# One of the four weight-block sums of each seven-product FFN pair: made by GpSimd instead of VectorE

## The chip, the core and the metric

The kernel runs on one core of one Trainium2 chip. The metric is the device time of one execution in microseconds (us). Engines go by their short names: PE is TensorE, which multiplies matrices (PEld is its weight load), DVE is VectorE, ACT is ScalarE, POOL is GpSimd, and SP is SyncE, which only issues transfers here.

## The reference, cut to what matters

The program is one layer of an encoder: 256 tokens, model width 2048, float32. After two kinds of attention comes a feed-forward network (FFN) with a gate, and it is the FFN that the change touches:

```
D_MODEL = 2048; SEQ = 256; D_FF = 5632
h = layer_norm(DEEPNORM_ALPHA * h + mixed, ln1_g[l], ln1_b[l])
ffn = jnp.einsum('bsf,fd->bsd', jax.nn.silu(jnp.einsum('bsd,df->bsf', h, w_gate[l]))
                 * jnp.einsum('bsd,df->bsf', h, w_up[l]), w_down[l])
h = layer_norm(DEEPNORM_ALPHA * h + ffn, ln2_g[l], ln2_b[l])
```

`w_gate` and `w_up` are 2048 x 5632, `w_down` is 5632 x 2048. All 5632 columns of gate and up, less one strip of 512 that is done ahead, belong to the part that the change touches.

## The kernel before, in words

**Products in two halves.** A float32 number is split into a rounded part (`hi`, type fp32r, made by ACT as a copy) and the rest (`lo`, made by DVE as the difference). A product of two float32 blocks is then three matmuls: hi by hi, hi by lo, lo by hi. So each weight block needs one ACT copy and one DVE subtraction before PE can use it.

**Units, groups and pairs.** The weights come in units of 128 rows x 1024 columns (`raw[u]`, half a MB, one SP transfer each). The FFN's gate and up matrices are walked in groups of 16 units: ("g", j) for gate and ("u", j) for up, j from 0 to 4, each 1024 columns wide. Within a group two neighbouring units make a pair, seen as 2 x 2 blocks of 128 x 512. Eight pairs make a group. A normal pair is eight products of three matmuls. In the four pairs of a group named by `SEVEN = (0, 2, 4, 6)` the 2 x 2 product is done in the manner of Strassen and Winograd with seven products instead of eight; these need sums of weight blocks first. There are 10 groups and so 40 seven-pairs in gate and up. The down projection (groups ("d", n)) comes behind them and has seven-pairs of its own.

**What a seven-pair asks of the engines** (`seven_parts(u)`; r1 and r2 are the two raw units):

- t1 (DVE): first half of the tile `s["t"]` = r1 left + r1 right, 128 x 512
- t3 (DVE): second half of `s["t"]` = r1 right + r2 right, 128 x 512
- lo11 (DVE, 512 columns), behind ACT's hi11
- t24 (DVE): two sums of 512 columns, the second on top of the first; the first reads t1's half alone
- lo2 (DVE, 1024 columns) behind ACT's split_hi of r2
- hi13 (ACT): one copy of both halves of `s["t"]`, 1024 columns; lo13 (DVE, 1024 columns) behind it
- hi24 (ACT) and lo24 (DVE), 1024 columns, for the t24 sums

A normal pair asks DVE for two `lo` of 1024 columns. At the end of a group DVE also joins the products out of PSUM (`ffn_ends`, `block_end`); for an "up" group it multiplies gate by up (tiles `s`), PE transposes the result, ACT copies it (`nb`) and POOL issues the transfer to `mid_d`.

**What sets the order.** Instructions are put out at build time by a planner: `Timed` keeps a modelled clock for each engine, and `next_part` gives the next ready part of a pair to the engine that its `op(...)` entry names. At run time each engine works through its list in order and waits for semaphores. What is ready early is kept in 46 slots of 4 KB per partition (tiles named `sl`). `Engine.__getattr__` issues every operation, so all of them carry line 53 in the profile.

Of the kernel before, what the change touches and what calls it, by code (L numbers as in the profile page):

```python
# [12 lines left out]
ALU = mybir.AluOpType  # L13
# [239 lines left out]
def layer_kernel(ctx: ExitStack, tc: tile.TileContext, A: dict, out: bass.AP):  # L253
    nc = Timed(tc.nc)
# [17 lines left out]
    def slot(shape, dt=F32):  # L272
        t = slab.tile(shape, dt, tag="slab", name=nm("sl"))
        if len(taken) + len(left_over) >= SLOTS and left_over:
            old = min(left_over, key=lambda x: nc.idle(x))
            left_over.remove(old)
            nc.follows(t, old)
        taken.append(t)
        return t
# [5 lines left out]
    def leave(*tiles):  # L285

        for t in tiles:
            taken.remove(t)
            left_over.append(t)
# [3 lines left out]
    def used(key, n, *tiles):  # L293

        uses[key] = uses.get(key, 0) + 1
        if uses[key] == n:
            leave(*tiles)
# [109 lines left out]
    def split_hi(u):  # L407
        wh[u] = slot([P, 1024], F32R)
        nc.scalar.activation(wh[u], raw[u], AF.Copy)

    def split_lo(u):
        wl[u] = slot([P, 1024], F32R)
        nc.vector.tensor_tensor(wl[u], raw[u], wh[u].bitcast(F32), op=ALU.subtract)
# [590 lines left out]
    def op(engine, fn, reads=(), after=(), early=False, takes=0):  # L1004


        return dict(engine=engine, fn=fn, reads=reads, after=after, early=early, takes=takes, done=False)
# [13 lines left out]
    def seven_parts(u):  # L1021

        r1, r2 = raw[u], raw[u + 1]
        s = sums[u] = {}

        def t1():
            s["t"] = slot([P, 2, 512])
            nc.vector.tensor_tensor(s["t"][:, 0], r1[:, :512], r1[:, 512:], op=ALU.add)

        def t3():  # L1030
            nc.vector.tensor_tensor(s["t"][:, 1], r1[:, 512:], r2[:, 512:], op=ALU.add)

        def hi11():
            s["b11"] = slot([P, 2, 512], F32R)
            nc.scalar.activation(s["b11"][:, 0], r1[:, :512], AF.Copy)

        def lo11():
            nc.vector.tensor_tensor(s["b11"][:, 1], r1[:, :512], s["b11"][:, 0].bitcast(F32), op=ALU.subtract)
            leave(r1)

        def hi13():
            s["hi"], s["lo"] = slot([P, 2, 512], F32R), slot([P, 2, 512], F32R)
            nc.scalar.activation(s["hi"], s["t"], AF.Copy)

        def lo13():
            nc.vector.tensor_tensor(s["lo"], s["t"], s["hi"].bitcast(F32), op=ALU.subtract)
            used(("t", u), 2, s["t"])

        def t24():
            s["u"] = slot([P, 2, 512])  # L1050
            nc.vector.tensor_tensor(s["u"][:, 0], s["t"][:, 0], r2[:, 512:], op=ALU.add)
            nc.vector.tensor_tensor(s["u"][:, 1], s["u"][:, 0], r2[:, :512], op=ALU.add)
            used(("t", u), 2, s["t"])
            used(("r2", u), 2, r2)

        def hi24():
            s[2], s[4] = slot([P, 2, 512], F32R), slot([P, 2, 512], F32R)
            nc.scalar.activation(s[2], s["u"], AF.Copy)

        def lo24():  # L1060
            nc.vector.tensor_tensor(s[4], s["u"], s[2].bitcast(F32), op=ALU.subtract)
            leave(s["u"])

        def lo2():
            split_lo(u + 1)
            used(("r2", u), 2, r2)

        return [
            op("act", hi11, lambda: [r1], takes=1),
            op("dve", t1, lambda: [r1], takes=1),  # L1070
            op("dve", t3, lambda: [r1, r2], (1,)),
            op("act", lambda: split_hi(u + 1), lambda: [r2], takes=1),
            op("dve", lo11, lambda: [s["b11"][:, 0]], (0, 1, 2)),
            op("act", hi13, lambda: [s["t"]], (1, 2), takes=2),
            op("dve", t24, lambda: [s["t"]], (1, 2), takes=1),
            op("dve", lo2, lambda: [wh[u + 1]], (3,), takes=1),
            op("act", hi24, lambda: [s["u"]], (6,), takes=2),
            op("dve", lo13, lambda: [s["hi"]], (5,)),
            op("dve", lo24, lambda: [s[2]], (8,)),
        ]  # L1080
# [54 lines left out]
    def is_down(u):  # L1135
        return units[u]["group"][0] == "d" and isinstance(units[u]["group"], tuple)
# [314 lines left out]
    def prepare(u, seven):  # L1451

        if u not in stages:
            stages[u] = seven_parts(u) if seven else one_parts(u)
            if splits_mid(u):
                add_mid_split(u, stages[u])
            if seven and is_down(u):
                add_mid_sums(u, stages[u])
        return stages[u]
# [165 lines left out]
```

## Time and profile before

| | us |
|---|---|
| time, median of 3 runs (1127.65 to 1128.34) | 1127.96 |
| profiled execution, its own time | 1127.88 |
| its span, first to last instruction | 1126.1 |
| PE busy | 1111.5 |
| DVE busy | 929.0 |
| ACT busy | 598.9 |
| POOL busy | 57.7 |

The span is the part of an execution that the trace covers; the profiled execution took 1.78 us more than its span. "Busy" adds up the time in which at least one instruction of the engine was running. The shares are means over stages that differ: the gate and up groups lie between about 452 and 856 us, the down projection behind them. The granted TensorE clock was 0.999 of full speed over the span, that is its upper level of 2.4 GHz.

### The profile page before, as it was taken

The page shows a single profiled execution, that of the slowest core. Times are in us where ns is not written, and L with a number is a line of the kernel's source. Part 1 is how long each engine was busy: PE and PEld are TensorE (multiplying, and loading weights), DVE is VectorE, ACT ScalarE, POOL GpSimd, SP SyncE. Part 2 cuts the span into 40 slices and gives each one's busy share as a digit, 9 for nine tenths or more (in the row PEclk, how much of TensorE's full clock was granted, in tenths as well). Part 3 has the DMA queues.
Part 4 walks back from the last instruction along what each step waited for, and adds up shares of the span by engine and source line. Part 5 has one row for each costly group of instructions (what it writes and reads, how often), then busy time and mean ns, then how long its engine had stood idle before and what let it go on. Part 6 is the DMA issues. An engine that isn't in the chain of part 4 may idle for free.

```text
span 1126.1 us, 14151 instructions
## 1 busy us (share of the span) xinstructions
PE 1111.5 (99%) x5032; PEld 904.7 (80%) x5032; DVE 929.0 (83%) x1263; ACT 598.9 (53%) x785; POOL 57.7 (5%) x110
## 2 busy tenths in 40 slices
PE   8999999999999999999999999999999999999998
PEld 4788888888788876888888888888888788878885
DVE  7863876547773669999999999999999999799865
ACT  5552656435563228656556556556567566446640
POOL 2000003110100020000000000000000000000000
PEclk9999999999999999999999999999999999999999
DMA  9664548795766754655754755755756877667741
GB/s 345 233 202 157 166 145 166 183 205 190 159 220 229 243 183 135 211 195 174 269 205 165 278 204 164 280 193 177 271 208 222 286 266 279 218 225 283 250 166 75
DMA packets 70407, 237.15 MB, mean 211 GB/s; under 512 B 8516, under 2 KB 9924, under 8 KB 70336
## 3 DMA queue, kind: packets, MB, share of 16 engines
q1 hardware_dynamic: 65008, 220.49, 57.2%
q0 software_dynamic: 5168, 15.68, 6.8%
q8 instruction: 39, 0.64, 0.2%
q14 instruction: 32, 0.26, 0.1%
q10 hardware_dynamic: 160, 0.08, 0.0%
HBM read 226.25 MB, written 9.97 MB: 210 GB/s over the span
## 4 chain that ended last, share of the span: by engine, by line
PE 49%; issue 41%; DVE 4%; ACT 2%; POOL 2%; DMA 1%; POOLq 0%; ACTq 0%; DVEq 0%
PE acc L53 49%; DVE sl L53 3%; POOL mid_d L53 1%; ACT sl L53 1%; DMA mid_d<-nb 1%; DVE stats L53 1%; ACT s L53 1%; DMA ident<-in_c_ident_dram 0%; DVE s L53 0%; POOL h_d L53 0%; POOL rs L53 0%; DMA sl<-in_w_out_dram 0%; POOL rstd L53 0%; ACT o L53 0%; DVE o L53 0%
## 5 line engine op out<-in xcount | busy, mean ns | idle before, releaser
L53 PE MATMUL acc<-sl,sl 128*128 128x512 f32 (+1 forms) x4676 | 1063.0, 388 | 2.3 <-DVE sl L53 1.4
L53 PEld LDWEIGHTS acc<-sl,sl 128*128 128x128 f32 x4676 | 860.5, 188 | 184.1 <-issue 6.2
L53 DVE TENSOR_TENSOR sl<-sl,sl 128x1024 fp32r<-128x1024 f32 (+3 forms) x710 | 683.1, 1017 | 44.9 <-ACT sl L53 36.6
L53 ACT ACTIVATE sl<-sl 128x1024 fp32r<-128x1024 f32 (+1 forms) x530 | 498.6, 994 | 272.8 <-DVE sl L53 140.8
L53 ACT ACTIVATE sl<-acc 128x256 fp32r<-128x256 f32 (+2 forms) x70 | 33.1, 497 | 91.0 <-PE acc L53 72.4
L53 DVE TENSOR_TENSOR sl<-acc,sl 128x256 fp32r<-128x256 f32 (+2 forms) x94 | 54.8, 596 | 28.2 <-ACT sl L53 21.5
L53 DVE TENSOR_TENSOR sl<-sl 128x512 f32<-128x512 f32 (+1 forms) x76 | 41.4, 558 | 0.3 <-PE acc L53 0.3
L53 DVE SCALAR_TENSOR_TENSOR sl<-sl,acc 128x512 f32<-128x512 f32 x10 | 6.8, 679 | 36.6 <-PE acc L53 36.6
L53 POOL DMA_DIRECT2D mid_d<-nb x22 | 11.9, 540 | 459.1 <-ACT nb L53 459.1
L53 ACT COPY sl<-acc 128x512 f32<-128x512 f32 x31 | 17.1, 588 | 34.3 <-PE acc L53 34.3
L53 ACT COPY nb<-acc 128x512 f32<-128x512 f32 x24 | 14.1, 588 | 35.1 <-PE acc L53 30.3
L53 DVE TENSOR_SCALAR sl<-acc 128x512 f32<-128x512 f32 x8 | 5.5, 688 | 32.7 <-PE acc L53 32.7
L53 ACT ACTIVATE s<-s 128x512 f32<-128x512 f32 x20 | 12.3, 631 | 23.5 <-DVE s L53 23.5
L53 ACT ACTIVATE s<-s,mx 128x256 f32<-128x256 f32 x32 | 15.9, 499 | 15.4 <-DVE mx L53 15.4
L53 POOL DMA_DIRECT2D nb<-in_na_rpb_dram x32 | 19.6, 621 | 85.7 <-DVE s L53 85.7
L53 PE MATMUL acc<-ident,s 128*128 128x128 f32 x136 | 20.5, 273 | 2.5 <-DVE s L53 1.7
L53 PEld LDWEIGHTS acc<-ident,s 128*128 128x128 f32 x136 | 16.5, 140 | 7.5 <-issue 1.9
L53 DVE TENSOR_TENSOR sl<-sl,acc 128x512 f32<-128x512 f32 x16 | 10.6, 681 | 12.7 <-PE acc L53 12.7
L53 PEld LDWEIGHTS acc<-ident,sl 128*128 128x128 f32 x128 | 15.2, 140 | 6.4 <-issue 4.5
L53 DVE BATCH_NORM_STATS2 stats<-sl 128x6 f32<-128x512 f32 x24 | 16.4, 692 | 3.2 <-DMA sl<-in_x_dram 2.6
L53 DVE SCALAR_TENSOR_TENSOR sl<-sl,rstd,sl 128x512 f32<-128x512 f32 x21 | 15.8, 752 | 3.5 <-POOL rstd L53 1.9
L53 DVE SCALAR_TENSOR_TENSOR sl<-sl,mv,sl 128x512 f32<-128x512 f32 x24 | 17.7, 745 | 0.2
(82 smaller groups left out, 226.2 us busy)
## 6 DMA issues: line engine op xcount, KB each, us to landing
sl<-in_w_in_dram SPq DMA_DIRECT2D x96, 512.0 KB, 4.8
sl<-in_w_down_dram SPq DMA_DIRECT2D x88, 512.0 KB, 5.8
sl<-in_w_gate_dram SPq DMA_DIRECT2D x80, 512.0 KB, 4.3
sl<-in_w_up_dram SPq DMA_DIRECT2D x80, 512.0 KB, 4.5
sl<-in_w_out_dram SPq DMA_DIRECT2D x32, 512.0 KB, 5.1
sl<-mid_d SPq DMA_DIRECT2D x14, 512.0 KB, 4.1
mid_d<-nb POOLq DMA_DIRECT2D x22, 256.0 KB, 3.4
sl<-in_w_gate_dram SPq DMA_DIRECT2D x16, 256.0 KB, 4.2
```

The lines of the kernel that those rows point to most:

```text
L53: result = getattr(self.engine, op)(*args, **kw)
```

## The change

t3 is issued on GpSimd for the pairs of gate and up, and stays on DVE for those of the down projection (`is_down(u)`). The planner is told so, and works out its order with its own cost for POOL.

```diff
         def t3():
-            nc.vector.tensor_tensor(s["t"][:, 1], r1[:, 512:], r2[:, 512:], op=ALU.add)
+            e = nc.vector if is_down(u) else nc.gpsimd
+            e.tensor_tensor(s["t"][:, 1], r1[:, 512:], r2[:, 512:], op=ALU.add)
...
             op("act", hi11, lambda: [r1], takes=1),
             op("dve", t1, lambda: [r1], takes=1),
-            op("dve", t3, lambda: [r1, r2], (1,)),
+            op("dve" if is_down(u) else "pool", t3, lambda: [r1, r2], (1,)),
```

Three places show what moves. First DVE's list for one seven-pair in the middle of a gate group (the third of group ("g", 1)); a row is one instruction, output <- inputs, with the buffers' numbers. Here is the list before, from t1 to the two `lo` of the normal pair behind it:

```order
L53 TENSOR_TENSOR sl_5210<-sl_5170 128x512
L53 TENSOR_TENSOR sl_5210<-sl_5170,sl_5172 128x512
L53 TENSOR_TENSOR sl_5208<-sl_5170,sl_5208 128x512
L53 TENSOR_TENSOR sl_5225<-sl_5210,sl_5172 128x512
L53 TENSOR_TENSOR sl_5225<-sl_5225,sl_5172 128x512
L53 TENSOR_TENSOR sl_5237<-sl_5172,sl_5212 128x1024
L53 TENSOR_TENSOR sl_5235<-sl_5210,sl_5234 128x1024
L53 TENSOR_TENSOR sl_5258<-sl_5225,sl_5257 128x1024
L53 TENSOR_TENSOR sl_5267<-sl_5204,sl_5246 128x1024
L53 TENSOR_TENSOR sl_5275<-sl_5206,sl_5248 128x1024
```

The rows are t1, t3, lo11, the two of t24, lo2, lo13, lo24 and the normal pair's two. The same place on DVE after the change:

```order
L53 TENSOR_TENSOR sl_5210<-sl_5171 128x512
L53 TENSOR_TENSOR sl_5208<-sl_5171,sl_5208 128x512
L53 TENSOR_TENSOR sl_5216<-sl_5210,sl_5173 128x512
L53 TENSOR_TENSOR sl_5216<-sl_5216,sl_5173 128x512
L53 TENSOR_TENSOR sl_5225<-sl_5173,sl_5213 128x1024
L53 TENSOR_TENSOR sl_5231<-sl_5210,sl_5230 128x1024
L53 TENSOR_TENSOR sl_5241<-sl_5216,sl_5240 128x1024
L53 TENSOR_TENSOR sl_5252<-sl_5204,sl_5250 128x1024
L53 TENSOR_TENSOR sl_5266<-sl_5206,sl_5254 128x1024
```

Only t3 is gone; the other nine keep their order. Second, POOL's list after the change, from the same pair to the first two pairs of the next gate group, where POOL also issues the transfers of the up group that has just ended:

```order
L53 TENSOR_TENSOR sl_5210<-sl_5171,sl_5173 128x512
L53 TENSOR_TENSOR sl_5292<-sl_5259,sl_5261 128x512
L53 TENSOR_TENSOR sl_5379<-sl_5341,sl_5343 128x512
L53 DMA mid_d<-nb_5453 128x512
L53 DMA mid_d<-nb_5502 128x512
L53 TENSOR_TENSOR sl_5508<-sl_5431,sl_5433 128x512
L53 DMA mid_d<-nb_5529 128x512
L53 DMA mid_d<-nb_5568 128x512
L53 TENSOR_TENSOR sl_5595<-sl_5547,sl_5549 128x512
```

Before, POOL had only the DMA rows there. Third, PE's list at the end of an up group, where the first of the four transposes (rows with `ident`, inputs are the `s` tiles that DVE has multiplied) stands among the next group's products. Before:

```order
L53 MATMUL acc_5443<-sl_5295,sl_3491 128x512
L53 MATMUL acc_5443<-sl_5313,sl_3491 128x512
L53 MATMUL acc_5443<-sl_5295,sl_3492 128x512
L53 MATMUL acc_5447<-sl_5295,sl_3592 128x512
L53 MATMUL acc_5447<-sl_5313,sl_3592 128x512
L53 MATMUL acc_5447<-sl_5295,sl_3592 128x512
L53 MATMUL acc_5451<-ident,s_5038 128x128 x4
```

And after the change:

```order
L53 MATMUL acc_5444<-sl_5295,sl_3491 128x512
L53 MATMUL acc_5444<-sl_5304,sl_3491 128x512
L53 MATMUL acc_5444<-sl_5295,sl_3492 128x512
L53 MATMUL acc_5448<-ident,s_5041 128x128 x4
L53 MATMUL acc_5456<-sl_5295,sl_3592 128x512
```

The transposes stand one product, three matmuls, earlier. PE's list is otherwise that of before, but for a few matmuls that trade places.

## Rows read from the trace of the kernel before

**Rows 1.** Busy time by stretch, two periods of gate and up; header names the columns

```profile
core 0: us, PE busy (x) PEld busy (x) DVE busy (x) ACT busy (x) POOL busy (x), PEclk, DMA share, GB/s
583.75:667.50 83.75, 83.75 (x378) 69.31 (x377) 82.11 (x100) 49.50 (x58) 2.16 (x4) 1.00 0.61 210
667.50:751.25 83.75, 83.75 (x378) 69.31 (x377) 82.10 (x99) 49.50 (x58) 2.16 (x4) 1.00 0.63 219
```

**Rows 2.** Waits between 452 and 856 us: in total, times, longest

```profile
POOL mid_d L53 <- ACT nb L53: 378.8, 18, 80.2
ACT sl L53 <- DVE sl L53: 93.7, 42, 4.4
...
DVE sl L53 <- ACT sl L53: 2.6, 5, 0.5
DVE sl L53 <- PE acc L53: 2.3, 5, 0.5
```

**Rows 3.** DVE's groups by shape, 500 to 835 us: count, busy, mean ns, idle before

```profile
L53 DVE TENSOR_TENSOR sl<-sl,sl 128x1024 fp32r<-128x1024 f32 x160 | 185.0, 1219 | 2.1 <-ACT sl L53 2.1
L53 DVE TENSOR_TENSOR sl<-sl,sl 128x512 f32<-128x512 f32 x97 | 66.6, 687 | 1.1
L53 DVE TENSOR_TENSOR sl<-acc,sl 128x512 f32<-128x512 f32 x24 | 16.5, 689 | 2.2 <-PE acc L53 2.0
L53 DVE TENSOR_TENSOR o<-acc,sl 128x512 f32<-128x512 f32 x16 | 11.0, 686 | 0.4
L53 DVE TENSOR_TENSOR s<-acc,sl 128x512 f32<-128x512 f32 x16 | 10.3, 683 | 0.1
```

**Rows 4.** DVE in order of time around one seven-pair: start, length, instruction

```profile
603.15 1.22 DVE L53 TENSOR_TENSOR sl<-sl,sl 128x1024 fp32r<-128x1024 f32 x1
604.29 0.69 DVE L53 TENSOR_TENSOR sl<-sl 128x512 f32<-128x512 f32 x1
604.89 8.29 DVE L53 TENSOR_TENSOR sl<-sl,sl 128x512 f32<-128x512 f32 x9
613.10 0.68 DVE L53 TENSOR_TENSOR sl<-sl 128x512 f32<-128x512 f32 x1
```

**Rows 5.** POOL in order of time, 0 to 20 us

```profile
0.72 0.52 POOL L53 MEMSET nb<- 128x512 f32 x1 [0.29 <-POOLq L1610]
1.18 0.10 POOL L53 MEMSET mhalf<- 128x1 f32 x1
```

**Rows 6.** All engines in order of time, 17.9 to 19.6 us

```profile
18.28 0.63 DVE L53 TENSOR_TENSOR sl<-acc,sl 128x512 fp32r<-128x512 f32 x1
...
18.45 0.19 POOL L53 TENSOR_SCALAR rstd<-mv 128x1 f32<-128x1 f32 x1 [8.11 <-DVE mv L53]
```

**Rows 7.** All engines in order of time, 404.2 to 406 us

```profile
404.57 0.75 DVE L53 SCALAR_TENSOR_TENSOR sl<-sl,mv,sl 128x512 f32<-128x512 f32 x1
404.63 0.74 POOL L53 TENSOR_SCALAR rstd<-mv 128x1 f32<-128x1 f32 x1 [56.39 <-DVE mv L53]
```

**Rows 8.** The same two instructions at 1106 us

```profile
1106.32 0.75 DVE L53 SCALAR_TENSOR_TENSOR sl<-sl,mv,sl 128x512 f32<-128x512 f32 x1
1106.37 0.74 POOL L53 TENSOR_SCALAR rstd<-mv 128x1 f32<-128x1 f32 x1 [78.98 <-DVE mv L53]
```

**Rows 9.** The end of an up group in order of time, 621.9 to 633.5 us

```profile
622.54 1.42 DVE L53 TENSOR_TENSOR sl<-acc,sl 128x512 f32<-128x512 f32 x2 [0.54 <-PE acc L53]
...
627.73 0.69 DVE L53 TENSOR_TENSOR s<-s,o 128x512 f32<-128x512 f32 x1
...
630.21 0.59 PEld L53 LDWEIGHTS acc<-ident,s 128*128 128x128 f32 x4
630.44 0.60 PE L53 MATMUL acc<-ident,s 128*128 128x128 f32 x4
630.46 0.68 DVE L53 TENSOR_TENSOR o<-acc,sl 128x512 f32<-128x512 f32 x1
630.76 2.84 PEld L53 LDWEIGHTS acc<-sl,sl 128*128 128x128 f32 x13
630.79 3.01 PE L53 MATMUL acc<-sl,sl 128*128 128x512 f32 x12
```

**Rows 10.** Groups by shape of the whole span, ACT and POOL

```profile
L53 ACT ACTIVATE sl<-sl 128x1024 fp32r<-128x1024 f32 x458 | 460.7, 1052 | 221.1 <-DVE sl L53 120.0 <-PE acc L53 47.4 <-DMA sl<-in_w_in_dram 20.8
L53 POOL DMA_DIRECT2D mid_d<-nb x22 | 11.9, 540 | 459.1 <-ACT nb L53 459.1
L53 POOL TENSOR_TENSOR rstd<-rstd,mhalf 128x1 f32<-128x1 f32 x5 | 3.2, 631 | 0.4
```

**Rows 11.** POOL and DVE in order of time, 631 to 643 us

```profile
631.95 0.54 POOL L53 DMA_DIRECT2D mid_d<-nb  x1 [72.54 <-ACT nb L53]
635.84 0.54 POOL L53 DMA_DIRECT2D mid_d<-nb  x1 [3.35 <-ACT nb L53]
639.09 0.54 POOL L53 DMA_DIRECT2D mid_d<-nb  x1 [2.71 <-ACT nb L53]
...
638.79 0.69 DVE L53 TENSOR_TENSOR sl<-sl 128x512 f32<-128x512 f32 x1
```

**Rows 12.** PE's waits in order of time, 880 to 900 and 1000 to 1126 us

```profile
888.88 0.66 PE L53 MATMUL acc<-ident,s 128*128 128x128 f32 x4 [0.78 <-ACT nb L53]
...
1004.65 1.46 PE L53 MATMUL acc<-sl,sl 128*128 128x512 f32 x4 [0.84 <-ACT sl L53]
1006.51 108.90 PE L53 MATMUL acc<-sl,sl 128*128 128x512 f32 x479 [0.40 <-DVE sl L53]
```

## The prediction

> **What bounds the kernel now.** I read busy time by stretch first, because the shares of the whole span mix stages. The gate and up groups repeat every 83.75 us (one gate and one up group, 8 seven-pairs), and in each such period PE is busy for all of its 83.75 us while DVE is busy for 82.1 of them [rows 1]. So PE sets the time here, and freeing another engine can't shorten the stage. But DVE is a close second: next I asked who waits for whom in this stage. DVE stood waiting for 2.6 us for ACT and 2.3 us for PE over five periods [rows 2], which is 4.9 / 5 = 0.98 us a period. The rest of its idle time, 83.75 - 82.1 - 0.98 = 0.67 us, lies in hand-overs between instructions that read their predecessor's result; I don't count it as spare. The question is therefore whether DVE gets lighter or heavier by the change, and where its lateness would first reach PE.
>
> The order of time shows the margin at that place. At the end of an up group DVE waits 0.54 us for PE's product, so it is right behind PE there; its first gate-by-up product ends at 627.73 + 0.69 = 628.42, and PE loads it as transposing weights at 630.21 [rows 9]. That is 1.79 us of margin, the smallest that I found in the period.
>
> **What is taken from DVE.** t3, 40 times. Its cost isn't its length of 687 ns [rows 3] but its place in the queue: t1 starts at 604.29 and t3 at 604.89 [rows 4], so back to back one such sum takes 0.60 us. Eight a period are 8 x 0.60 = 4.80 us.
>
> **What is added on POOL.** 40 sums of two SBUF inputs of 512 columns. No row shows POOL doing one, so I bound it. The writing of 512 columns took 0.52 us and of one column 0.10 [rows 5]: (0.52 - 0.10) / 511 = 0.82 ns a column for one stream, 0.42 us for 512. A one-column operation that reads took 0.19 us when nothing was in its way [rows 6]. If POOL took both inputs and the output at once, t3 would take 0.19 + 0.42 = 0.61 us; if the two inputs come one after the other, 0.19 + 0.84 = 1.03 us; if all three streams follow each other, 0.19 + 1.26 = 1.45 us. The one two-input operation in the trace, of one column, averages 0.63 us [rows 10], but it is a power, not a sum. I take 1.03 and keep 0.61 and 1.45. POOL itself has room: 2.2 us busy in a period [rows 1].
>
> **Does POOL's work cost DVE anything?** This decides the case. Rows 7 and 8 show that the two engines are in each other's way. A POOL operation on one column that takes 0.19 us beside a DVE instruction with one input in PSUM [rows 6] takes 0.74 us when DVE has started, some 0.05 us earlier, an instruction with two wide SBUF inputs [rows 7, 8]; it ends at 404.63 + 0.74 = 405.37, and DVE's at 405.32; at 1106 us again 1107.11 and 1107.07. So POOL got nothing until DVE's two-input instruction had ended. The trace doesn't show the reverse, DVE behind a long POOL read. Its bounds are nothing, if only POOL waits, and POOL's whole length, if whoever comes first keeps the way. I take the whole length, since what shows in rows 7 and 8 is a way held for a whole instruction by the one that was first. DVE can hardly avoid it: of the DVE instructions of the gate and up stage only the 24 + 16 + 16 = 56 that read PSUM between 500 and 835 us [rows 3] are of another kind, about 4 x 100 = 400 are run there [rows 1].
>
> The Trainium skill's page "SBUF — State Buffer", section "Who interferes with whom", states the same as a rule for both directions: VectorE with two SBUF inputs and GpSimd reading SBUF exclude each other, and the later one blocks until the first has ended. The trace agrees for POOL's side, 0.74 instead of 0.19 us; no run here shows DVE's side. The page "GPSIMD Engine Reference", section 3.1, has 4497 ns for a sum over 2048 columns; a quarter of it is an estimate of 1.12 us for t3, and the sum below would give 1143 us by it.
>
> **The sum.** A period adds 8 x 1.03 = 8.24 us of standing to DVE and takes 4.80 us from it. DVE's own waits, 0.98 us, swallow part of the rest: 8.24 - 4.80 - 0.98 = 2.46 us a period that DVE is later than PE needs. Over five periods that is 12.3 us. The margin in front of the transposes covers some of it once: 1.79 us, less the 0.68 us by which the change puts them earlier (three matmuls; PE's 12 in 3.01 us [rows 9] start about 0.23 apart), leaves 1.1. So PE loses 12.3 - 1.1 = 11.2 us. The profiled execution took 1127.88 us, within 0.1 of the median of the runs, 1127.96; so I forecast 1127.88 + 11.2 = 1139 us. DVE breaks even at a hold of (4.80 + 0.98) / 8 = 5.78 / 8 = 0.72 us, and the loss passes 0.2%, about 2.3 us and what a measurement of this kernel can tell from no change, at ((2.3 + 1.1) / 5 + 5.78) / 8 = 0.81 us. With 1.45 us a period adds 11.6 - 5.78 = 5.82, five 29.1, less 1.1: 1156 us. With 0.61 nothing is lost.
>
> **What is moved past what.** t3 waits on POOL for t1 and for both loads. t24 doesn't wait for it; ACT's hi13 does, and lo13 behind that. From t1's start to lo13's DVE has t1, lo11, both of t24 at 0.60 and lo2 at 604.29 - 603.15 = 1.14 us [rows 4], 3.5 us, and the hold on top. t3 needs t1's 0.6, the rest of the DVE instruction that has the way (0.6), its own 1.03, and hi13's 1.05 [rows 10], with about 0.1 for each of two hand-overs: 3.5 us. Since DVE's chain also stretches by the hold, about 1 us is left and lo13 costs no wait. ACT behind hi13 waits a good deal for DVE anyway, 93.7 us in the stage [rows 2]. On POOL t3 stands between transfers to mid_d that wait for ACT's copies [rows 2]; an issue takes 0.54 us [rows 10]. In a gate group's first pair two transfers stand ahead of t3; they went out at 631.95 and 635.84, before that pair's t1 at 638.79 [rows 11]. I price this at nothing; should it cost 0.54 us each period, it is 5 x 0.54 = 2.7 us at most. PE's other moved matmuls and SP's unchanged list cost nothing: PE is never short of ready products there.
>
> **Rivals.**
> - *Only POOL waits.* DVE takes the way whenever it asks, and t3 slips into the moments when DVE hands over between dependent instructions or reads PSUM. For it: rows 7 and 8 show just this direction. Against it: there DVE came first. DVE would then be 4.80 us lighter a period, PE is as busy as before, and the time stays at 1128. It decides if DVE's rows next to t3 keep their lengths, that is if the hold is under 0.72 us. A gain could come only from PE's waits behind the stage, 0.78 + 0.84 + 0.40 = 2.0 us [rows 12], so at best 1126.
> - *The hold is heavier*, by more than 1.45 us. POOL's fixed part may be nearer the 0.63 us of its only two-input row [rows 10] than 0.19: 0.63 + 1.26 = 1.89 us. Then a period adds 15.1 - 5.78 = 9.3 us, five 46.7, less 1.1: 1173 us.
> - *t3 comes too late for lo13.* If DVE's back-to-back stream lets POOL in only after lo2, DVE stands at lo13 for t3 and hi13, 1.03 + 1.05 + 0.2 = 2.3 us: 18.4 - 5.78 = 12.6 us a period, some 1190 us. Against it: between the two t24 DVE waits for its own result, and POOL can start there.
>
> **How the numbers follow.** The forecast, a hold between 0.81 and 1.45 us, gets 0.68; only POOL waits, or the hold is shorter, 0.21; the heavier hold 0.08; the late t3 0.03. Of the 0.21 I put 0.03 below 1125.6, since PE's 2.0 us are all there is, and 0.18 within 0.2%. Slower is then 0.68 + 0.08 + 0.03 = 0.79. The range has to take in a good part of "only POOL waits" at its low end, 1127, and the three-stream bound at its high end, 1156; outside lie about 0.08 below and 0.11 above. The forecast's own range is 1131 to 1156.
>
> **What the profile after would show.** In the gate and up stage: POOL rows of 128x512 of about 1 us, longer where they had to wait; eight DVE rows a period stretched by up to 1 us or so, though their shapes are as before; DVE busy close to the whole period; PE waiting for DVE, first at the transposes of the up groups and then at the weight blocks; and a period of 83.75 + 2.46 = 86.2 instead of 83.75 us. The down projection should keep its length. I am wrong if the DVE rows beside t3 keep 0.69 and 1.22 us, or if POOL's rows are under 0.7 us; and wrong in size if the period grows by far more or less than 2.5 us.

## The result and the profile after

The changed kernel takes 1137.19 us (1136.79 to 1138.32), the kernel before in the same session 1127.81: a ratio of 1.0082, 95% interval 1.0069 to 1.0095. It is 9.4 us slower; 11.2 were forecast. The profiled execution has a span of 1136.5 us against 1126.1, so 10.4 us more.

First where the time went. Two stretches of the trace before, busy time by stretch (columns as in [rows 1]): the gate and up groups, and all that follows.

```profile
452.00:856.00 404.00, 404.00 (x1818) 334.28 (x1817) 396.36 (x474) 240.33 (x282) 9.72 (x18) 1.00 0.62 214
856.00:1126.00 270.00, 262.81 (x1151) 213.73 (x1149) 232.71 (x304) 138.39 (x156) 5.65 (x11) 1.00 0.65 228
```

The same two pieces of work in the changed kernel:

```profile
452.00:866.40 414.40, 408.19 (x1819) 333.59 (x1818) 409.08 (x434) 239.62 (x282) 79.65 (x57) 1.00 0.62 209
866.00:1136.50 270.50, 263.48 (x1150) 213.54 (x1149) 234.05 (x305) 139.36 (x156) 5.68 (x11) 1.00 0.66 228
```

The whole loss lies in the gate and up stage, 404.0 to 414.4 us with the same PE work (1819 matmuls against 1818). DVE has 40 instructions fewer there (434 against 474) and is busy for 12.7 us more. One period, which answers to [rows 1]:

```profile
588.00:673.88 85.88, 84.43 (x378) 68.96 (x377) 84.77 (x91) 49.23 (x58) 15.55 (x12) 1.00 0.61 208
673.88:759.76 85.88, 84.35 (x377) 68.88 (x377) 84.78 (x91) 49.20 (x58) 16.48 (x12) 1.00 0.62 209
```

The first transposes of the up groups show how long a period is: [rows 9] has them at 630.44 us, and a period later, before (first row) and in the changed kernel (second row, after 633.32) they stand at

```profile
713.98 0.60 PE L53 MATMUL acc<-ident,s 128*128 128x128 f32 x4
...
719.20 0.66 PE L53 MATMUL acc<-ident,s 128*128 128x128 f32 x4 [0.48 <-DVE s L53]
```

So a period has become 85.88 us long instead of 83.54; the stretches of 83.75 us in [rows 1] were a little longer than a period. PE is idle for 1.5 us of the 85.88, DVE is busy for 84.8.

Why DVE is busier with less to do shows in order of time. The first two rows are from DVE's list in the changed kernel, the third from POOL's at the same place:

```profile
788.22 1.22 DVE L53 TENSOR_TENSOR sl<-sl,sl 128x1024 fp32r<-128x1024 f32 x1
789.36 1.78 DVE L53 TENSOR_TENSOR sl<-sl 128x512 f32<-128x512 f32 x1
...
788.55 2.04 POOL L53 TENSOR_TENSOR sl<-sl,sl 128x512 f32<-128x512 f32 x1 [11.81 <-DMA sl<-in_w_gate_dram]
```

POOL starts t3 at 788.55, while DVE is in a `lo` of 1024 columns that runs its usual 1.22 us, to 789.44. POOL's sum lasts until 790.59. DVE's next instruction, a t1 that took 0.69 us in [rows 4], takes 1.78: it ends at 791.14, 0.55 us behind POOL. As such a sum takes 0.60 us back to back, nearly all of its 512 columns went through only after POOL's sum had ended. First POOL stood behind DVE, then DVE behind POOL, 1.10 us longer. Another t3 stood beside DVE instructions that read PSUM:

```profile
593.12 1.89 DVE L53 TENSOR_TENSOR s<-acc,sl 128x512 f32<-128x512 f32 x3
...
593.57 1.30 POOL L53 TENSOR_TENSOR sl<-sl,sl 128x512 f32<-128x512 f32 x1 [7.83 <-PE acc L53]
```

Here POOL takes 1.30 us, its time when nothing is in the way, and DVE's three joins take 1.89 us together, as much as before (0.68 each, overlapping by 0.08). This happens once in each of the five periods. By shape, DVE's groups between 500 and 840 us, to set beside [rows 3]:

```profile
L53 DVE TENSOR_TENSOR sl<-sl,sl 128x1024 fp32r<-128x1024 f32 x159 | 213.4, 1401 | 2.1 <-ACT sl L53 2.1
L53 DVE TENSOR_TENSOR sl<-sl,sl 128x512 f32<-128x512 f32 x64 | 43.9, 686 | 1.1
L53 DVE TENSOR_TENSOR sl<-acc,sl 128x512 f32<-128x512 f32 x24 | 16.4, 684 | 0.3
L53 DVE TENSOR_TENSOR o<-acc,sl 128x512 f32<-128x512 f32 x16 | 10.9, 684 | 0.0
L53 DVE TENSOR_TENSOR s<-acc,sl 128x512 f32<-128x512 f32 x16 | 10.3, 684 | 0.4
```

The mean of the 1024-column `lo` has gone from 1219 to 1401 ns; groups that read PSUM (`acc`) have kept theirs. A mean hides that most rows are unchanged and some are 1.1 us longer, so I counted the rows beside POOL's 40 sums (the first starts at 446 us): 35 DVE rows are more than 0.15 us longer than their shape's usual length, by 38.8 us in all; the middle one is 1.10 us longer.

Last, the waits between 452 and 866 us, to set beside [rows 2]; all the waits of PE, PEld and DVE in that stretch but one of 0.2 us:

```profile
PEld acc L53 <- DVE s L53: 6.4, 9, 0.9
PEld acc L53 <- DVE o L53: 5.4, 4, 1.4
PE acc L53 <- DVE o L53: 3.6, 4, 0.9
DVE sl L53 <- ACT sl L53: 2.6, 5, 0.5
PE acc L53 <- DVE s L53: 2.2, 5, 0.5
```

DVE's waits for PE, 2.3 us before, are gone, and PE waits for DVE instead. In order of time this is at the end of the up groups, at the transposes and at the next accumulation, which needs a PSUM bank that DVE's join (`o`) has to empty:

```profile
633.32 0.66 PE L53 MATMUL acc<-ident,s 128*128 128x128 f32 x4 [0.48 <-DVE s L53]
...
636.98 3.02 PE L53 MATMUL acc<-sl,sl 128*128 128x512 f32 x12 [0.90 <-DVE o L53]
```

### The profile page after: what moved, and what is told of

The parts are those of the page before. It is cut to its first block, busy times and chain, and to the rows that moved or that the text cites. A ratio compares the mean times of both kernels' runs of the same rounds, so it can differ in the third digit from the quotient of the medians.

```text
span 1136.5 us, 14273 instructions
## 1 busy us (share of the span) xinstructions
PE 1116.6 (98%) x5032; PEld 903.6 (79%) x5032; DVE 942.9 (83%) x1223; ACT 599.2 (53%) x785; POOL 130.2 (11%) x150
## 5 line engine op out<-in xcount | busy, mean ns | idle before, releaser
L53 DVE TENSOR_TENSOR sl<-sl,sl 128x1024 fp32r<-128x1024 f32 (+2 forms) x670 | 694.4, 1089 | 41.8 <-ACT sl L53 38.1
L53 POOL TENSOR_TENSOR sl<-sl,sl 128x512 f32<-128x512 f32 x40 | 72.2, 1804 | 266.5 <-PE acc L53 130.0
L53 DVE SCALAR_TENSOR_TENSOR sl<-sl,acc 128x512 f32<-128x512 f32 x10 | 6.8, 678 | 36.6 <-PE acc L53 36.6
L53 POOL DMA_DIRECT2D nb<-in_na_rpb_dram x32 | 19.6, 620 | 85.8 <-DVE s L53 85.7
L53 PEld LDWEIGHTS acc<-ident,s 128*128 128x128 f32 x136 | 16.1, 140 | 10.4 <-DVE s L53 4.7
L53 POOL TENSOR_SCALAR rstd<-mv 128x1 f32<-128x1 f32 x5 | 2.6, 522 | 157.8 <-DVE mv L53 157.8
```

The source lines that it names most:

```text
L53: result = getattr(self.engine, op)(*args, **kw)
```

## The experiments

Two theories were to be told apart. **Load**: POOL's reading holds DVE, and DVE becomes what sets the stage. **Plan**: the planner, told of POOL, puts out another order at the end of the up groups (transposes one product earlier; one lo13 between the joins), and that order makes PE wait, whatever POOL does. PE's waits above stand just where the order has changed, so the profile alone doesn't decide. A variant of load, that t3 comes late from POOL and holds up ACT, is tried by the fourth run. In the edits `nc.nc` issues an instruction without the planner's clock, and `nc.note` tells the planner of one; so plan and engine can be set apart.

**e1: POOL writes but doesn't read** (t3's sum is left out of the computation, a memset stands in its place; plan and lists of the changed kernel):

```diff
-            e.tensor_tensor(s["t"][:, 1], r1[:, 512:], r2[:, 512:], op=ALU.add)
+            nc.nc.gpsimd.memset(s["t"][:, 1], 0.0)
+            nc.note("pool", "tensor_tensor", [s["t"][:, 1]], [r1[:, 512:], r2[:, 512:]])
```

> The changed kernel's plan and lists, but in place of t3 POOL only writes the 512 columns (a memset): no reading of SBUF, and the sum itself is left out of the computation. Load theory (POOL's reading holds DVE for about 1.1 us, seven times in eight, and DVE is then what sets the gate and up stage): nothing holds DVE, DVE is 4.8 us a period lighter than before, PE bounds again: 1126 to 1129 us, DVE rows at 0.69 and 1.22 us. Plan theory (the planner's other order at the end of the up groups, transposes one product earlier and one lo13 between the joins, makes PE wait some 2 us a period): about 1137 us as in the changed kernel.

1127.65 us, ratio to the kernel before 0.9995 (0.9986 to 1.0004). No DVE row is lengthened. The busy times of a stretch of [rows 1] and DVE's largest waits (452 to 856 us):

```profile
583.75:667.50 83.75, 83.75 (x379) 69.31 (x378) 77.28 (x92) 49.84 (x58) 6.39 (x12) 1.00 0.63 215
```

```profile
DVE sl L53 <- PE acc L53: 23.2, 9, 3.4
```

Plan falls: with the same order PE is busy for all of its 83.75 us. And most of the 4.8 us that DVE gains a period comes back as waits: 77.3 us busy, and 23.2 us of waiting for PE where there were 2.3. Relieving DVE alone is worth nothing here.

**e2: the changed plan, but DVE does t3** (POOL does nothing new):

```diff
-            e = nc.vector if is_down(u) else nc.gpsimd
-            e.tensor_tensor(s["t"][:, 1], r1[:, 512:], r2[:, 512:], op=ALU.add)
+            nc.nc.vector.tensor_tensor(s["t"][:, 1], r1[:, 512:], r2[:, 512:], op=ALU.add)
+            nc.note("dve" if is_down(u) else "pool", "tensor_tensor", [s["t"][:, 1]], [r1[:, 512:], r2[:, 512:]])
```

> The changed kernel's plan with t3 done by DVE, at the place in DVE's list where the plan puts it out; POOL does nothing new. All other lists are those of the changed kernel. Load theory: DVE's load is that of before, so 1127 to 1131 us, at most 2 us of waits of the order's own. Plan theory: 1136 to 1138 us.

1128.03 us, ratio 0.9998 (0.9990 to 1.0007): the order by itself costs nothing that can be measured.

**e3: the old plan, but POOL does t3** (every list of the kernel before, with t3 taken out of DVE's and put into POOL's):

```diff
-            nc.vector.tensor_tensor(s["t"][:, 1], r1[:, 512:], r2[:, 512:], op=ALU.add)
+            e = nc.nc.vector if is_down(u) else nc.nc.gpsimd
+            e.tensor_tensor(s["t"][:, 1], r1[:, 512:], r2[:, 512:], op=ALU.add)
+            nc.note("dve", "tensor_tensor", [s["t"][:, 1]], [r1[:, 512:], r2[:, 512:]])
```

> The plan and all lists of the kernel before, but t3 of gate and up is done by POOL instead of DVE. Load theory: the hold is there, 1134 to 1139 us, with DVE rows of about 2.3 us beside t3. Plan theory: 1127 to 1129 us.

1136.35 us, ratio 1.0072 (1.0058 to 1.0086). Without any change of order nearly the whole loss is there, with 33 lengthened DVE rows (36.6 us). PE's weight loads now wait at the transposes alone:

```profile
PEld acc L53 <- DVE s L53: 8.4, 5, 2.1
```

So the order only chooses at which of DVE's late results PE stands.

**e4: DVE keeps its t3, POOL does the same sum once more** into a tile that nobody reads (bf16):

```diff
             nc.vector.tensor_tensor(s["t"][:, 1], r1[:, 512:], r2[:, 512:], op=ALU.add)
+            if not is_down(u):
+                nc.nc.gpsimd.tensor_tensor(spare, r1[:, 512:], r2[:, 512:], op=ALU.add)
```

> The kernel before with DVE's t3 kept, and POOL doing the same sum of the same two inputs once more for each of the 40 pairs, into a tile that nobody reads. No instruction of another engine waits for it but the loads that reuse the slots. Load theory: DVE is held 1.1 us seven times in eight, 40 x 1.1 x 7/8 = 38 us, less some 2 us of DVE's own waits and 1.8 us of margin: about 1162 us (1155 to 1172). Plan theory, or any theory in which t3's lateness on POOL and not the hold costs the time: 1127 to 1129 us.

1164.34 us, ratio 1.0316 (1.0302 to 1.0330), 36.7 us more than before. Nobody waits for POOL's result here, and every instruction of the kernel before is still in its place; so it is the hold that costs, not a late t3. The loads that reuse the two raw units now wait for POOL's reading as well, but the waits of PE, PEld, DVE and ACT for a load come to 0.2 us from 452 to 893 us. 39 DVE rows are lengthened, by 41.9 us.

**e5 and e6: the same place, but a POOL copy with one input, and a POOL memset.**

```diff
-                nc.nc.gpsimd.tensor_tensor(spare, r1[:, 512:], r2[:, 512:], op=ALU.add)
+                nc.nc.gpsimd.tensor_copy(spare, r1[:, 512:])
...
-                nc.nc.gpsimd.tensor_tensor(spare, r1[:, 512:], r2[:, 512:], op=ALU.add)
+                nc.nc.gpsimd.memset(spare, 0.0)
```

> The kernel before, with a POOL copy of one SBUF input (512 columns of r1) added for each of the 40 pairs, into a tile that nobody reads. If what holds DVE is POOL's reading, one stream holds about half as long as two, some 0.5 us: 40 x 0.5 x 7/8 = 17.5 us, less 2.3 us of DVE's own waits and 1.8 us of margin: about 1141 us (1134 to 1147). If only a POOL instruction with two inputs holds DVE: 1127 to 1129 us. If any POOL instruction that reads holds it for its whole length as the sum does: up to 1160 us.

> The kernel before, with a POOL memset of 512 columns added for each of the 40 pairs, into a tile that nobody reads. Reading is what holds: 1127 to 1129 us. If POOL's writing held DVE too, for its 0.4 to 0.5 us: 40 x 0.45 x 7/8 = 16 us, less 4.1 us: about 1140 us.

The copy: 1138.01 us, ratio 1.0093 (1.0078 to 1.0109). The memset: 1127.40 us, ratio 0.9998 (0.9989 to 1.0007). Two rows of the run with the copy, DVE's t1 and the POOL copy before it:

```profile
685.85 1.10 DVE L53 TENSOR_TENSOR sl<-sl 128x512 f32<-128x512 f32 x1
...
684.90 1.51 POOL L1034 CAST spare<-sl 128x512 bf16<-128x512 f32 x1 [10.10 <-DMA sl<-in_w_up_dram]
```

The t1 is 0.41 us longer than usual; 38 rows are longer, by 15.5 us in all. With the memset none is, though all 40 memsets run beside DVE instructions that read SBUF (they wait for no load, so they come earlier than the sums). Reading from SBUF is what holds DVE, and one input holds it for 0.41 us where two hold it for 1.10.

**e7: t3 on POOL in two of a group's four seven-pairs.**

```diff
+    def by_dve(u):
+        return is_down(u) or units[u]["k"] // 2 in (0, 4)
...
-            e = nc.vector if is_down(u) else nc.gpsimd
+            e = nc.vector if by_dve(u) else nc.gpsimd
...
-            op("dve" if is_down(u) else "pool", t3, lambda: [r1, r2], (1,)),
+            op("dve" if by_dve(u) else "pool", t3, lambda: [r1, r2], (1,)),
```

> The changed kernel with t3 on POOL in only two of a group's four seven-pairs (the second and the fourth), on DVE in the others; the planner is told. Load theory, by the balance of a period: DVE loses 4 x 0.60 = 2.4 us of work and is held 3 or 4 times 1.10 us, 3.3 to 4.4 us; less the 0.46 us that it waited for PE, it is 0.4 to 1.5 us late a period, and less the margin in front of the transposes (1.1 to 1.8 us) PE loses 0.5 to 6 us: 1128 to 1134 us, at any rate under half of the changed kernel's loss of 9.4 us plus 1.3. If the loss were in proportion to the number of moved sums, with no threshold: 1127.9 + 4.7 = 1132.6 us.

1128.54 us, ratio 1.0007 (0.9998 to 1.0015): no change that can be told, and not half the loss. 14 DVE rows are lengthened by 13.5 us, which is 1.5 more than the 12.0 us (20 x 0.60) that DVE no longer does. Half of the sums is here far less than half of the load: six of the 20 hold nothing. In the changed kernel the same difference is 38.8 - 24.0 = 14.8 us. The 1.5 us are swallowed: DVE's waits for PE in the stage go from 2.3 to 0.9 us.

```profile
DVE sl L53 <- PE acc L53: 0.9, 3, 0.4
```

**One balance for all.** For each run: what the lengthened rows add, less what DVE no longer does, less DVE's waits for PE in the stage before (2.3 us) and the margin in front of the transposes (1.8 us by the old plan, 1.1 by the new); all in us, beside the median's distance from the kernel before.

| run | rows | added | taken | cover | balance | measured |
|---|---|---|---|---|---|---|
| changed kernel | 35 | 38.8 | 24.0 | 3.4 | 11.4 | 9.4 |
| e2, plan only | 0 | 0 | 0 | 3.4 | none | 0.4 |
| e3, old plan | 33 | 36.6 | 24.0 | 4.1 | 8.5 | 8.8 |
| e4, extra sum | 39 | 41.9 | 0 | 4.1 | 37.8 | 36.7 |
| e5, extra copy | 38 | 15.5 | 0 | 4.1 | 11.4 | 10.5 |
| e6, extra memset | 0 | 0 | 0 | 4.1 | none | -0.1 |
| e7, two of four | 14 | 13.5 | 12.0 | 3.4 | none | 1.0 |
| e1, memset | 0 | 0 | 24.0 | 3.4 | none | 0.1 |

The balance comes within 2.0 us everywhere (for the changed kernel within 1.0 of the 10.4 us by which the profiled span grew; its rows are from that execution). No run beat the kernel before, and e1 shows that none of this kind could: with DVE's load lowered by the full 24 us PE still needs its time.

## Why the prediction was right

- **PE bounds the stage, DVE is a close second, a lighter DVE gains nothing.** Right; e1 shows it.
- **The hold.** Right in kind and in the choice of bound: a two-input DVE instruction that comes after POOL's sum waits for it. "Only POOL waits" falls by e4. The Trainium skill's page "SBUF — State Buffer", section "Who interferes with whom", has this for both directions, and also that one that only writes doesn't contend; the runs agree (1.78 instead of 0.69 us beside the sum, no lengthened row with the memsets). The Trainium skill's wording, that whoever is first has the way for the whole instruction, is a little more than most rows show: unhindered, POOL's sum took 1.30 us (the profile's spans on POOL are rough), and where POOL had first stood behind DVE, DVE was held 1.10. Four rows come near it, with 1.25 us:

```profile
564.60 2.47 DVE L53 TENSOR_TENSOR sl<-sl,sl 128x1024 fp32r<-128x1024 f32 x1
564.68 1.30 POOL L53 TENSOR_TENSOR sl<-sl,sl 128x512 f32<-128x512 f32 x1
```

- **Its size.** 1.03 us was forecast and 1.10 measured, but not for the reasons given. The estimate was for the whole POOL instruction, which takes 1.30. And two inputs hold 2.7 times as long as one (1.10 to 0.41), not twice. The estimate from the Trainium skill's page "GPSIMD Engine Reference", section 3.1, a quarter of its figure for 2048 columns, was 1.12, nearer to the hold than to the instruction.
- **How often.** All eight sums of a period were charged; seven hold, and the eighth stands beside DVE's joins out of PSUM. The prediction saw that those don't collide but took no account of it: 7 x 1.10 = 7.7 us a period instead of 8.24.
- **DVE's own waits.** Of the 0.98 us a period that was set against the hold, only the half that DVE waited for PE was there to be used; the 2.6 us for ACT are still there after the change. 7.7 - 4.80 - 0.46 = 2.4 us a period; measured 85.88 - 83.54 = 2.34. Eight holds instead of seven, at 1.03 instead of 1.10, were 0.5 us too much, and the waits set against them 0.5 us too much as well: that 2.46 came so close is luck.
- **Where PE stands.** At the transposes first, as forecast. But then not at the weight blocks: at PSUM banks that DVE's joins empty late. No wait for a weight block (`sl`) is left among PE's waits.
- **t3 in time for lo13.** Right: DVE's waits for ACT are 2.6 us as before, so POOL's lateness costs DVE no wait. In e4, where nobody needs POOL's sum, the loss follows the hold all the same.
- **The down projection keeps its length.** Right: 270.0 and 270.5 us.

One reading and two labels are wrong, and the prediction's sum hangs on none of them. A period before is 83.54 us long, not 83.75, so the forecast growth of 2.46 us would have made it 86.0. The seven-pair of [rows 4] and of the lists in the section on the change is the fourth of group ("u", 1), not the third of ("g", 1), and the pair of [rows 11], called the first in the prediction, is the third of its gate group, as is the first t3 behind two transfers in the POOL list.

What was seen and not tried on purpose: t3 beside PSUM joins costs nothing. In the five runs in which POOL reads (the changed kernel, e3, e4, e5 and e7), 21 of its 180 sums and copies lengthened no DVE row by more than 0.15 us, and each of the 21 lay beside a DVE instruction that reads PSUM. But no run moved sums there to gain from it.

## What to carry to other kernels

Before moving a sum from VectorE to GpSimd, look at what VectorE runs meanwhile. If its instructions read two SBUF inputs back to back, GpSimd's sum takes VectorE's time anyway: here 1.10 us for each 0.60 us that it saved. Only beside instructions that read PSUM was it free. And a second engine that is 98% busy can take a little more and then no more: 1.5 us of added work (e7) cost nothing that can be told, 14.8 us (the changed kernel) cost 9.4. So read how much it waits, and for whom, before adding to it; here its waits for the engine that bounds the kernel were used up, its waits for a third stayed.

## What was not expected of the hardware

- A POOL copy of 512 columns from one input holds DVE 0.41 us, a sum of two inputs 1.10 us; a memset, 0.53 us long, not at all.
- Which of the two comes first isn't settled by who asks first once. At 564.60 above, DVE's row begins 0.08 us before POOL's, and DVE is the one that is held. In the changed kernel a t3 took up to 2.55 us, of which only 1.30 is its own; in that one (453.72 us) DVE ran three short instructions before POOL got in. The first extra sum of e4 stood far longer, while DVE started 14 instructions that read SBUF and POOL got in only when DVE waited for a result of its own:

```profile
436.32 11.78 POOL L1034 TENSOR_TENSOR spare<-sl,sl 128x512 bf16<-128x512 f32 x1 [15.33 <-DMA sl<-in_w_gate_dram]
```

What decides it stays open. Had a t3 stood so long, the prediction's third rival, a t3 too late for lo13, could have come true.

- In e4 the granted clock of PE fell in parts of the stage, beside PE's waits for DVE of up to 3.9 us at a time:

```profile
600.00:700.00 100.00, 93.76 (x391) 74.64 (x392) 98.35 (x110) 55.04 (x66) 15.35 (x12) 0.93 0.54 182
700.00:800.00 100.00, 96.22 (x429) 78.62 (x429) 98.87 (x109) 56.46 (x67) 17.92 (x13) 1.00 0.58 198
```

0.93 is a mean of a stretch, mostly at 2.4 GHz and partly at 1.2. DVE was busy for 98% of it, and the balance, which leaves the clock out, is no less than the measured loss (37.8 and 36.7 us); so no cost of the lower clock shows.
